# Trunk step in emulated fp32: norms in pairs of PSUM tiles, both statistics first, two output products in one step, a later mean

## The chip, the cores and the metric

The kernel runs on one core of one Trainium2 chip. The metric is device microseconds of one execution. Two other times occur: the *span* is the stretch of the profiled execution that the trace covers, and the time of that same execution is a little longer than its span. Engines are called by short names: PE (TensorE), DVE (VectorE), ACT (ScalarE), POOL (GpSimd), SP (SyncE, which issues the DMAs). L126 is line 126 of the kernel before.

## The reference

One layer of a decoder trunk on 1072 tokens (16 meta tokens, 1024 of a prompt, 8 x 4 new ones), 1024 channels wide, and then a last RMSNorm:

```python
def hybrid_layer(x, conv_prev, pool_prev, pos0, ...):
    x = x + 0.5 * swiglu(rmsnorm(x, g1), w1g, w1u, w1d)
    h = rmsnorm(x, gm)
    z = h @ w_in + b_in
    u = z[..., :C_CONV] * jax.nn.sigmoid(z[..., C_CONV:2 * C_CONV])
    p_in = z[..., 2 * C_CONV:]
    ...
    c = depthwise_causal_conv(u_ext, w_dw, b_dw)
    c = jax.nn.silu(layernorm(c, ln_g, ln_b))
    ...
    q = multiscale_pool(p_ext, pos0, w_pool, pool_scale)
    x = x + jnp.concatenate([c, q], axis=-1) @ w_out + b_out
    x = x + 0.5 * swiglu(rmsnorm(x, g2), w2g, w2u, w2d)
```

The hidden width of the SwiGLUs is 2816, the convolution is 31 wide and causal, the pools are trailing means over 2, 4, 8 and 16 positions, each with a 128 x 128 map. All is float32.

## The kernel before

**Layout.** Channels lie on the 128 partitions, tokens along the free dimension, so every product has weights as the stationary side and tokens as the moving side. The tokens are cut into three pieces of 358 columns, X1, X2 and X3 (tiles x_61, x_62 and x_4993 in the program's order; shorter where the padding of two columns, or the 16 meta tokens, are left away: 356 and 340). A number is held as a high and a low part, and each product is three matmuls (`mul`, L126): weight high by data high, weight high by data low, weight low by data high. `split` makes the two parts: ACT casts to the high part (L143), DVE subtracts it to get the low part (L144; POOL does this for weights, `wl`).

**PSUM.** One pool has eight banks, each an `acc` tile of 128 x 512. Matmul groups take them, and so do the norms, whose scaled tile lies in a bank between L265 and L144. A tile can be taken when the last instruction that reads its bank's earlier holder has run.

**Order.** PE's instructions run in the order in which the program writes them. The program is a plan of steps (one or a few products each, with weights fetched ahead through queues of raw and split tiles). Norms, mixings and operand sums are generators in the background: after each step of the plan `run_background` advances them by 1.8 of their `yield`s for each estimated microsecond of PE work; a `yield LAG` stops the front one until that much estimated PE time has gone by. A step that needs a generator's result runs it to its end at once (`got`, `finish`). Within DVE, ACT and POOL a scheduler sets the order from this program.

**The stages, and the generators that run beside them.** (1) first FFN of X1 and X2 together (a fast form with seven products in place of eight); (2) first FFN of X3, plain: beside it the norm `h1b` ahead of it, the norm `hma` of X1 and X2 for the first mixing, that mixing's input products (`proj_in`), its convolution, LayerNorm and pools (`mixer`), its output products (`proj_out`), and the norm `h2a`; (3) second FFN of X1 (340 columns), plain: beside it the norm `hmb` of X3 and the second mixing on X3, then `s2`, the operands of (4), the fast second FFN of X2 and X3, with seven operand pairs (b11, b21, t2, t3, t1, t4, b22) made by `fast_operands`; (5) the last norm.

**A norm** (`normed`) of a piece: squares on ACT, their adds on DVE (`square_sum`, L237), on PE a sum over partitions, an inverse root by small operations on DVE (`rsqrt`, L199 to L205), three diagonal tiles (L208, `diag`) which PE spreads over the partitions, a copy of that (`nr`, L217), and then for each of 8 channel tiles a scaled tile in PSUM (L265) and its split (L143, L144). Other names: `smt`, `mixl`, `mixh` and `mixlt` are the split results of norms and mixings, `hid0` to `hid2` hidden tiles of the FFNs, L489 the add of a down product to x, L515 a gate times its up product, L859 the LayerNorm's scaling and L843 its sum over channel tiles.

In the second mixing `conv_group` sums the convolution's channels, runs the pools, waits for LAG4 and then issues the mean's matmul (`mean_of`).

Of the kernel before, what the change touches and what calls it, by code (L numbers as in the profile page):

```python
# [2 lines left out]

# [9 lines left out]
ALU = mybir.AluOpType  # L13
# [40 lines left out]
LAG3 = 6.0  # L54
LAG4 = 7.0
LAG5 = 20.0
LAG6 = 4.0
POOL = {'b1': (1, 3), 't4': (0, 1, 2, 3), 't3': (0, 1, 2, 3), 't2': (1, 3), 'sq': ()}
W_BUFS = 6
T_BUFS = 6  # L60
# [24 lines left out]
def trunk(ctx: ExitStack, tc: tile.TileContext, xt, wf1, win, wout, wf2, wpool, vec, eye, sconv, spool,  # L85
# [34 lines left out]
    def accum():  # L120
        return pp.tile([P, 512], F32, name="acc", tag="acc")
# [19 lines left out]

    def split(hi, lo, src, engine=None):
        nc.scalar.copy(hi, src)  # L143
        (engine or nc.vector).tensor_tensor(lo, src, hi, ALU.subtract)  # L144


    raw_list = []
# [28 lines left out]
    def both_parts(w, k):  # L176

        wh, wl = w[k // KH]
        return wh[:, k % KH], wl[:, k % KH]
# [61 lines left out]
    def rms(piece, out):  # L241
        s = yield from square_sum([X(k, piece) for k in range(KD)])
        yield LAG
        out[piece] = yield from rsqrt(s, 1.0 / D, EPS)
# [19 lines left out]
    def scaled(t, piece, k, gain, r):  # L264
        nc.vector.scalar_tensor_tensor(t, X(k, piece), col(gain, k), r, ALU.mult, ALU.mult)  # L265

    def normed(pieces, gain, tiles, out, stats=None):

        st = {} if stats is None else stats
        h, lo = tiles()  # L270
        at = 0
        for piece in pieces:
            n = piece[1] - piece[0]
            if piece not in st:
                yield from rms(piece, st)
            for k in range(KD):
                t = accum()[:, :n]
                scaled(t, piece, k, gain, st[piece])
                yield
                split(h[:, k, at : at + n], lo[:, k, at : at + n], t)  # L280
                yield
            at += n
        out["h"] = (h, lo)
# [536 lines left out]
    def conv_group(piece, a0, cb, ch, cl, between, after):  # L820


        n = piece[1] - piece[0]
        npr = min(piece[1], END_PROMPT) - piece[0]
        if npr < n:
            us = mix["us"]
            taps = vecs[:, COL["w_dw"] : COL["w_dw"] + C_TILES * TAPS].rearrange("p (m k) -> p m k", m=C_TILES)
            cs = cb[:, :, npr:n].rearrange("p m (b t) -> p m b t", b=DEC_B)
            for t in range(DEC_T):
                for m in range(C_TILES):  # L830
                    pr = const.tile([P, DEC_B, TAPS], F32, name="pr", tag="tmp", bufs=T_BUFS)
                    nc.vector.tensor_tensor(pr, us[:, m, :, t : t + TAPS],  # L832
                                            taps[:, m : m + 1, :].broadcast_to([P, DEC_B, TAPS]), ALU.mult)
                    nc.vector.tensor_reduce(cs[:, m, :, t], pr, mybir.AxisListType.X, ALU.add)
                    yield
            for m in range(C_TILES):
                nc.vector.tensor_scalar(cb[:, m, npr:n], cb[:, m, npr:n], col("b_dw", m), None, ALU.add)
            yield
        s = const.tile([P, N], F32, name="ns", tag="ns")[:, :n]
        part = accum()[:, :n]  # L840
        nc.scalar.copy(part, cb[:, 0, :n])
        for m in (1, 2, 3):
            nc.vector.tensor_tensor(s if m == 3 else part, part, cb[:, m, :n], ALU.add)  # L843
            yield
        yield from between()
        yield LAG4
        mu = mean_of(s, 1.0 / (C_TILES * P), 0.0)
        yield
        for m in range(C_TILES):
            nc.vector.tensor_tensor(cb[:, m, :n], cb[:, m, :n], mu, ALU.subtract)  # L850
            yield
        s = yield from square_sum([cb[:, m, :n] for m in range(C_TILES)])
        yield LAG3
        yield from after()
        st = {}
        yield from rsqrt(s, 1.0 / (C_TILES * P), EPS, st, False)
        for m in range(C_TILES):
            t = accum()[:, :n]
            nc.vector.tensor_tensor(t, cb[:, m, :n], st["psum"], ALU.mult)  # L859
            nc.scalar.activation(t, t, AF.Silu, bias=col("ln_b", m), scale=col("ln_g", m))  # L860
            yield
            split(ch[:, m], cl[:, m], t)
            yield
# [67 lines left out]

    def proj_out(pieces, key):

        out = []
        for m in range(KD):
            def use(w, m=m):
                accs = [accum()[:, : b - a] for a, b in pieces]
                for what, ks in (("pool", range(C_TILES, KD)), ("h", range(C_TILES))):
                    h, lo = got(key, what)()
                    mul(accs, [(*both_parts(w, k), h[:, k], lo[:, k]) for k in ks], what == "pool", what == "h")  # L940
                for acc, piece in zip(accs, pieces):
                    nc.vector.scalar_tensor_tensor(X(m, piece), acc, col("b_out", m), X(m, piece), ALU.add, ALU.add)
            out.append(plain(wout[m], use))
        return out

    def store(piece, k, t):
# [446 lines left out]
```

## Time and profile before

| what | value |
|---|---|
| time, median of 3 runs | 1804.93 us (1803.71 to 1805.00) |
| time of the profiled execution | 1803.07 us |
| its span | 1801.3 us |
| granted TensorE clock, mean | 0.986 |
| PE busy | 1729.7 us (96%) |
| DVE busy | 1378.4 us (77%) |
| POOL busy | 1146.0 us (64%) |
| ACT busy | 760.3 us (42%) |

A busy time is the time in which the engine has an instruction in execution; its share is of the span. In a timeline, the first number is the start in microseconds from the span's start, the second how long the instruction (or a run of like ones, "x7") took, and brackets at the end hold the idle time of the engine ahead of it and the instruction that ended it. PEclk in a window is the granted clock as a share of full speed.

### The profile page before, as it was taken

Reading aid. Unit: us, or ns where it says so; the run is one execution under the profiler, and the core shown is the slowest. Engines: PE = TensorE matmul, PEld = TensorE weight load, DVE = VectorE, ACT = ScalarE, POOL = GpSimd, SP = SyncE. Lnnn points to the kernel's source line nnn. Section 1 sums busy time; section 2 is a strip of 40 time slices with the busy share of each in tenths; the row PEclk is TensorE's granted clock in tenths of the full one; section 3 lists DMA queues with packets and bytes.
Section 4 is the critical chain, followed back from the end, with each engine's and each line's share of the span. In section 5 each row is a group of like instructions: output and inputs, shape, how many; then the busy total and the mean of one; then the engine's idle time right before and its main releaser. Section 6 shows DMA issues by size and latency. Waiting matters only on the chain.

```text
span 1801.3 us, 29876 instructions
## 1 busy us (share of the span) xinstructions
PE 1729.7 (96%) x10486; PEld 1712.5 (95%) x10486; DVE 1378.4 (77%) x2621; ACT 760.3 (42%) x1482; POOL 1146.0 (64%) x894
## 2 busy tenths in 40 slices
PE   6799999999999999999999998999999999999997
PEld 6799999999999999999999998999999999999997
DVE  8869898989747795897235888538587989898965
ACT  6444444443435224434234433545353434444444
POOL 5576766667745337667346657666577676767683
PEclk9899999999999999999999999999999999999998
DMA  6122232223353223443234494444332222222232
GB/s 209 35 83 71 71 103 82 72 77 98 103 118 119 65 67 115 124 135 111 66 106 129 126 135 133 126 134 123 111 105 91 71 83 71 82 71 72 70 100 83
DMA packets 115893, 177.70 MB, mean 99 GB/s; under 512 B 28320, under 2 KB 35744, under 8 KB 115744
## 3 DMA queue, kind: packets, MB, share of 16 engines
q1 hardware_dynamic: 115744, 175.80, 33.4%
q8 instruction: 83, 1.36, 0.3%
q14 instruction: 66, 0.54, 0.1%
HBM read 170.60 MB, written 5.15 MB: 98 GB/s over the span
## 4 chain that ended last, share of the span: by engine, by line
PE 75%; DVE 17%; issue 4%; DMA 2%; POOL 1%; ACT 1%; SPq 0%; DVEq 0%; POOLq 0%; ACTq 0%
PE acc L126 75%; DMA wraw<-in_wf 2%; DVE acc L265 2%; POOL wl L144 1%; DVE acc L814 1%; DVE wraw L542 1%; DVE acc L570 1%; DVE wraw L541 1%; DVE tmp L570 1%; DVE tmp L692 1%; DVE x L489 1%; DVE tmp L265 1%; DVE pr L832 1%; DVE wraw L543 0%; DVE xb L144 0%
## 5 line engine op out<-in xcount | busy, mean ns | idle before, releaser
L144 POOL TENSOR_TENSOR wl<-wraw,wh 128x512 fp32r<-128x512 f32 x740 | 991.3, 1350 | 588.9 <-ACT wh L143 541.7
L143 ACT CAST wh<-wraw 128x512 fp32r<-128x512 f32 x740 | 453.6, 621 | 685.6 <-PE acc L126 455.5
L126 PE MATMUL acc<-smt,wh 128*128 128x358 f32 x1024 | 253.1, 328 | 5.0 <-DVE mixl L144 4.0
L126 PEld LDWEIGHTS acc<-smt,wh 128*128 128x128 f32 x1024 | 181.7, 190 | 6.3 <-DVE mixl L144 4.6
L814 DVE SCALAR_TENSOR_TENSOR acc<-ub,vecs,acc 128x340 f32<-128x340 f32 (+2 forms) x348 | 183.5, 571 | 2.6
L126 PE MATMUL acc<-mixlt,wh 128*128 128x340 f32 x704 | 165.6, 319 | 2.6 <-DVE smt L144 2.4
L126 PE MATMUL acc<-smt,wl 128*128 128x358 f32 x512 | 167.8, 328 | 0.0
L489 DVE SCALAR_TENSOR_TENSOR x<-acc,x 128x358 f32<-128x358 f32 (+1 forms) x240 | 119.4, 517 | 35.0 <-PE acc L126 34.2
L618 DVE SCALAR_TENSOR_TENSOR x<-acc,x 128x358 f32<-128x358 f32 x320 | 145.0, 516 | 0.5 <-PE acc L126 0.4
L570 DVE TENSOR_TENSOR acc<-tmp,acc 128x358 f32<-128x358 f32 x168 | 85.7, 527 | 51.5 <-PE acc L126 48.2
L126 PEld LDWEIGHTS acc<-mixlt,wh 128*128 128x128 f32 x704 | 120.9, 188 | 3.4 <-DVE smt L144 2.7
L126 PE MATMUL acc<-mixlt,wl 128*128 128x340 f32 x352 | 112.1, 319 | 0.8 <-POOL wl L144 0.8
L144 POOL TENSOR_TENSOR wl<-sx,wh 128x512 fp32r<-128x512 f32 x58 | 85.5, 1475 | 30.5 <-ACT wh L143 28.7
L126 PEld LDWEIGHTS acc<-smt,wl 128*128 128x128 f32 x512 | 96.9, 189 | 0.0
L542 DVE TENSOR_TENSOR wraw<-sx,wraw 128x512 f32<-128x512 f32 x58 | 78.1, 1347 | 11.8 <-POOL wl L144 11.6
L126 PE MATMUL acc<-mixh,wh 128*128 128x356 f32 (+1 forms) x320 | 79.3, 328 | 4.7 <-DVE mixl L144 2.7
L126 PE MATMUL acc<-mixl,wh 128*128 128x356 f32 (+1 forms) x320 | 78.6, 327 | 0.0
L126 PE MATMUL acc<-mixh,wl 128*128 128x356 f32 (+1 forms) x320 | 78.5, 327 | 0.0
L541 DVE TENSOR_TENSOR wraw<-wraw 128x512 f32<-128x512 f32 x58 | 77.0, 1327 | 0.4
L570 DVE TENSOR_TENSOR tmp<-tmp,acc 128x358 f32<-128x358 f32 x126 | 65.4, 519 | 14.3 <-PE acc L126 13.1
L126 PE MATMUL acc<-b11h,wh 128*128 128x358 f32 x184 | 61.7, 335 | 10.8 <-ACT wh L143 10.8
L543 DVE TENSOR_TENSOR wraw<-wraw 128x512 f32<-128x512 f32 x58 | 70.4, 1214 | 2.0 <-POOL wl L144 1.5
(286 smaller groups left out, 4762.1 us busy)
## 6 DMA issues: line engine op xcount, KB each, us to landing
wraw<-in_wf SPq DMA_DIRECT2D x544, 256.0 KB, 2.9
wraw<-in_win SPq DMA_DIRECT2D x48, 256.0 KB, 2.7
wraw<-in_wout SPq DMA_DIRECT2D x32, 256.0 KB, 2.9
x<-in_xt SPq DMA_DIRECT2D x8, 179.0 KB, 4.3
tmp<-in_xt SPq DMA_DIRECT2D x8, 179.0 KB, 2.8
x<-in_xt SPq DMA_DIRECT2D x1, 1432.0 KB, 7.0
x<-in_xt SPq DMA_DIRECT2D x8, 178.0 KB, 5.0
out_yt<-tmp SPq DMA_DIRECT2D x8, 170.0 KB, 3.3
```

Of the source, the lines that this page charges most:

```text
L126: tc.keep_in_program_order(nc.tensor.matmul(acc, lhs, rhs, start=start, stop=stop))
L143: nc.scalar.copy(hi, src)
L144: (engine or nc.vector).tensor_tensor(lo, src, hi, ALU.subtract)
L265: nc.vector.scalar_tensor_tensor(t, X(k, piece), col(gain, k), r, ALU.mult, ALU.mult)
L489: nc.vector.scalar_tensor_tensor(X(m, piece), acc, 0.5, X(m, piece), ALU.mult, ALU.add)
L541: nc.vector.tensor_tensor(a21, a11, a21, ALU.subtract)
L542: nc.vector.tensor_tensor(a11, s1, a11, ALU.subtract)
L543: nc.vector.tensor_tensor(a12, a12, a11, ALU.subtract)
L570: nc.vector.tensor_tensor(t, s, acc, ALU.add)
L618: nc.vector.scalar_tensor_tensor(to, acc, 0.5 * sign, to, ALU.mult, ALU.add)
L692: sub(t, t, ops[name][1][i], ALU.subtract)
L814: nc.vector.scalar_tensor_tensor(to, src, w, part, ALU.mult, ALU.add)
```

## The change

Four edits, none of which changes what is computed or how many instructions there are. (1) `normed` calls a new `rms_all`, which makes the statistics of all its pieces ahead of any scaled tile, and issues the first piece's `diag` matmul right after the second piece's squares; each scaled tile is queued on DVE behind the low part of two tiles before (`issue_after` sets an order within an engine and waits for nothing itself). (2) `proj_out` takes the first two output products in one step: pool parts of both, then the parts of the convolution group (`h`) of both. (3) In the second mixing the wait ahead of the mean's matmul is 14 and not 7 of estimated PE time. (4) The wait between two blocks of `fast_operands` is 9 and not 4. The new lines move later ones by 1, 2, 16 or more: L144 becomes L145, L208 becomes L209, L237 becomes L238, L265 becomes L266, L489 becomes L505 and L515 becomes L531.

```diff
-LAG6 = 4.0
+LAG6 = 9.0
+LAG7 = 14.0
...
     def split(hi, lo, src, engine=None):
         nc.scalar.copy(hi, src)
-        (engine or nc.vector).tensor_tensor(lo, src, hi, ALU.subtract)
+        return (engine or nc.vector).tensor_tensor(lo, src, hi, ALU.subtract)
...
+    def rms_all(pieces, out):
+
+        steps, last = None, None
+        for piece in pieces:
+            s = yield from square_sum([X(k, piece) for k in range(KD)])
+            if steps is not None:
+                out[last] = whole(steps)
+            yield LAG
+            steps, last = rsqrt(s, 1.0 / D, EPS), piece
+            next(steps)
+        if steps is not None:
+            yield LAG2
+            out[last] = whole(steps)
+
     def normed(pieces, gain, tiles, out, stats=None):
+
 
         st = {} if stats is None else stats
         h, lo = tiles()
-        at = 0
+        yield from rms_all([piece for piece in pieces if piece not in st], st)
+        at, lows = 0, []
         for piece in pieces:
             n = piece[1] - piece[0]
-            if piece not in st:
-                yield from rms(piece, st)
             for k in range(KD):
                 t = accum()[:, :n]
-                scaled(t, piece, k, gain, st[piece])
+                with tc.issue_after(lows[-2].ins) if len(lows) > 1 else nullcontext():
+                    scaled(t, piece, k, gain, st[piece])
                 yield
-                split(h[:, k, at : at + n], lo[:, k, at : at + n], t)
+                lows.append(split(h[:, k, at : at + n], lo[:, k, at : at + n], t))
                 yield
...
         yield from between()
-        yield LAG4
+        yield LAG4 if npr == n else LAG7
         mu = mean_of(s, 1.0 / (C_TILES * P), 0.0)
...
     def proj_out(pieces, key):
 
-        out = []
-        for m in range(KD):
-            def use(w, m=m):
-                accs = [accum()[:, : b - a] for a, b in pieces]
-                for what, ks in (("pool", range(C_TILES, KD)), ("h", range(C_TILES))):
-                    h, lo = got(key, what)()
-                    mul(accs, [(*both_parts(w, k), h[:, k], lo[:, k]) for k in ks], what == "pool", what == "h")
+
+        def products(w, m, accs, what, ks):
+            h, lo = got(key, what)()
+            mul(accs, [(*both_parts(w, k), h[:, k], lo[:, k]) for k in ks], what == "pool", what == "h")
+
+        def use(ws, ms):
+            banks = [[accum()[:, : b - a] for a, b in pieces] for _ in ms]
+            for what, ks in (("pool", range(C_TILES, KD)), ("h", range(C_TILES))):
+                for w, m, accs in zip(ws, ms, banks):
+                    products(w, m, accs, what, ks)
+            for m, accs in zip(ms, banks):
                 for acc, piece in zip(accs, pieces):
                     nc.vector.scalar_tensor_tensor(X(m, piece), acc, col("b_out", m), X(m, piece), ALU.add, ALU.add)
-            out.append(plain(wout[m], use))
+
+        out = []
+        for ms in ((0, 1), *((m,) for m in range(2, KD))):
+            out.append(("step", [[(0, wout[m])] for m in ms], lambda ms=ms: [unit() for _ in ms],
+                        lambda ws, ms=ms: use(ws, ms), False))
         return out
```

The rows of order that follow are the program's, without time; `x3` is a run of three like instructions.

DVE, norm `hmb` of X3 in the second mixing, from its diagonal tiles on, before:

```order
L208 TENSOR_SCALAR diag<-ident,few 128x128 x3
L489 SCALAR_TENSOR_TENSOR x_61<-acc,x_61 128x340 x3
L265 SCALAR_TENSOR_TENSOR acc<-x_4993,vecs,nr 128x358 x7
L144 TENSOR_TENSOR smt<-acc,smt 128x358 x7
L265 SCALAR_TENSOR_TENSOR acc<-x_4993,vecs,nr 128x358
L144 TENSOR_TENSOR smt<-acc,smt 128x358
L515 TENSOR_TENSOR acc<-acc,tmp 128x340
```

and of the change, the same place (the alternation goes on in this way to the eighth tile):

```order
L209 TENSOR_SCALAR diag<-ident,few 128x128 x3
L505 SCALAR_TENSOR_TENSOR x_61<-acc,x_61 128x340 x3
L266 SCALAR_TENSOR_TENSOR acc<-x_4993,vecs,nr 128x358 x2
L145 TENSOR_TENSOR smt<-acc,smt 128x358
L266 SCALAR_TENSOR_TENSOR acc<-x_4993,vecs,nr 128x358
L145 TENSOR_TENSOR smt<-acc,smt 128x358
L266 SCALAR_TENSOR_TENSOR acc<-x_4993,vecs,nr 128x358
L145 TENSOR_TENSOR smt<-acc,smt 128x358
```

Seven scaled tiles stood in a row before the first low part; now two do. The norms `hma` and `h2a` are changed in the same way.

DVE, norm `hma`, the first piece's root, while down products of X3 (`hid`) run on PE; before:

```order
L489 SCALAR_TENSOR_TENSOR x_4993<-acc,x_4993 128x358
L204 TENSOR_TENSOR acc<-acc,few 128x3
L205 SCALAR_TENSOR_TENSOR few<-acc,few 128x3
L489 SCALAR_TENSOR_TENSOR x_4993<-acc,x_4993 128x358
L208 TENSOR_SCALAR diag<-ident,few 128x128 x3
L489 SCALAR_TENSOR_TENSOR x_4993<-acc,x_4993 128x358 x3
L265 SCALAR_TENSOR_TENSOR acc<-x_61,vecs,nr 128x356 x7
L144 TENSOR_TENSOR mixl<-acc,mixh 128x356 x7
```

and of the change:

```order
L238 TENSOR_TENSOR acc<-acc,tmp 128x358
L205 TENSOR_TENSOR acc<-acc,few 128x3
L505 SCALAR_TENSOR_TENSOR x_4993<-acc,x_4993 128x358
L238 TENSOR_TENSOR ns<-acc,tmp 128x358
L206 SCALAR_TENSOR_TENSOR few<-acc,few 128x3
L204 SCALAR_TENSOR_TENSOR acc<-acc,few 128x3
L205 TENSOR_TENSOR acc<-acc,few 128x3
L206 SCALAR_TENSOR_TENSOR few<-acc,few 128x3
L204 SCALAR_TENSOR_TENSOR acc<-acc,few 128x3
L205 TENSOR_TENSOR acc<-acc,few 128x3
L206 SCALAR_TENSOR_TENSOR few<-acc,few 128x3
L209 TENSOR_SCALAR diag<-ident,few 128x128 x3
```

The square-adds of the second piece (L238) now stand ahead of the root's last operations and of its diagonal tiles, and the next x adds behind them.

PE at the same root, before:

```order
L126 MATMUL acc<-hid1h,wh 128x358
L126 MATMUL acc<-hid1l,wh 128x358
L126 MATMUL acc<-hid1h,wl 128x358
L126 MATMUL acc<-diag,ones 128x128 x3
L126 MATMUL acc<-smt,wh 128x358 x2
L126 MATMUL acc<-smt,wl 128x358
L126 MATMUL acc<-smt,wh 128x358 x2
```

and of the change:

```order
L127 MATMUL acc<-hid1h,wh 128x358
L127 MATMUL acc<-hid1l,wh 128x358
L127 MATMUL acc<-hid1h,wl 128x358
L127 MATMUL acc<-diag,ones 128x128 x3
L127 MATMUL acc<-hid0h,wh 128x358
L127 MATMUL acc<-hid0l,wh 128x358
```

The `diag` matmul stood at the end of the second half of the down products and stands now between the two halves: 24 matmuls earlier. The second piece's `diag` matmul stood 130 rows behind the first's, and stands 74 rows behind it.

DVE, operands of the second fast FFN, second block, up to the first x add of a down product; before:

```order
L144 TENSOR_TENSOR t2l<-acc,t2h 128x358
L329 TENSOR_TENSOR acc<-tmp,acc 128x358
L318 TENSOR_TENSOR tmp<-tmp,acc 128x358
L319 TENSOR_TENSOR acc<-acc,tmp 128x358
L265 SCALAR_TENSOR_TENSOR tmp<-x_62,vecs,nr 128x358
L144 TENSOR_TENSOR b11l<-tmp,b11h 128x358
L144 TENSOR_TENSOR b22l<-tmp,b22h 128x358
L265 SCALAR_TENSOR_TENSOR tmp<-x_62,vecs,nr 128x358
L515 TENSOR_TENSOR acc<-acc,tmp 128x340
L489 SCALAR_TENSOR_TENSOR x_61<-acc,x_61 128x340
```

and of the change:

```order
L145 TENSOR_TENSOR t2l<-acc,t2h 128x358
L345 TENSOR_TENSOR acc<-tmp,acc 128x358
L145 TENSOR_TENSOR b11l<-tmp,b11h 128x358
L145 TENSOR_TENSOR b22l<-tmp,b22h 128x358
L266 SCALAR_TENSOR_TENSOR acc<-x_4993,vecs,nr 128x358
L531 TENSOR_TENSOR acc<-acc,tmp 128x340
L145 TENSOR_TENSOR t4l<-acc,t4h 128x358
L505 SCALAR_TENSOR_TENSOR x_61<-acc,x_61 128x340
```

From the `hid1l` ahead of this stretch to that x add 22 instructions stood between; now 19 do.

## Rows read from the trace of the kernel before

**Rows 1.** The page: busy time by engine; costliest groups (busy us, mean ns).

```profile
PE 1729.7 (96%) x10486; PEld 1712.5 (95%) x10486; DVE 1378.4 (77%) x2621; ACT 760.3 (42%) x1482; POOL 1146.0 (64%) x894
...
L143 ACT CAST wh<-wraw 128x512 fp32r<-128x512 f32 x740 | 453.6, 621 | 685.6 <-PE acc L126 455.5
```

**Rows 2.** Timeline of PE: start, busy us, instruction, [idle before, releaser].

```profile
555.80 0.60 PE L126 MATMUL acc<-smt,wh 128*128 128x358 f32 x2 [2.20 <-DVE mixl L144]
...
587.59 0.86 PE L126 MATMUL acc<-mixh,wh 128*128 128x356 f32 x2 [2.66 <-DVE mixl L144]
...
947.31 0.60 PE L126 MATMUL acc<-smt,wh 128*128 128x358 f32 x2 [1.06 <-DVE mixlt L144]
...
996.78 0.58 PE L126 MATMUL acc<-mixlt,wh 128*128 128x340 f32 x2 [2.40 <-DVE smt L144]
```

**Rows 3.** Timeline of DVE, norm of the second mixing's tiles.

```profile
991.16 5.13 DVE L265 SCALAR_TENSOR_TENSOR acc<-x,vecs,nr 128x358 f32<-128x358 f32 x7 [0.65 <-ACT nr L217]
...
996.20 3.14 DVE L144 TENSOR_TENSOR smt<-acc,smt 128x358 fp32r<-128x358 f32 x7
```

**Rows 4.** Windows: length, busy PE, PEld, DVE, ACT, POOL; PEclk, DMA, GB/s.

```profile
588.00:592.00 4.00, 3.99 (x17) 3.97 (x17) 3.54 (x8) 0.90 (x2) 1.05 (x1) 0.65 0.25 81
...
997.00:1001.00 4.00, 4.00 (x27) 4.00 (x27) 3.47 (x9) 2.02 (x5) 2.74 (x2) 1.00 0.42 126
...
1244.00:1248.00 4.00, 3.33 (x12) 3.33 (x13) 4.00 (x10) 1.66 (x4) 2.27 (x2) 0.57 0.31 82
```

**Rows 5.** Timeline of PE, where the first mixing's root is due.

```profile
544.90 0.32 PE L126 MATMUL acc<-hid0h,wh 128*128 128x358 f32 x1
...
548.85 0.83 PE L126 MATMUL acc<-diag,ones 128*128 128x128 f32 x6
```

**Rows 6.** Timeline of DVE around that root, and square-adds behind it.

```profile
541.05 0.17 DVE L199 TENSOR_SCALAR acc<-acc 128x3 f32<-128x3 f32 x1
541.26 0.17 DVE L200 TENSOR_SCALAR acc<-acc 128x3 int32<-128x3 int32 x1
...
545.10 0.53 DVE L489 SCALAR_TENSOR_TENSOR x<-acc,x 128x358 f32<-128x358 f32 x1 [0.19 <-PE acc L126]
...
546.53 0.92 DVE L208 TENSOR_SCALAR diag<-ident,few 128x128 f32<-128x128 f32 x3
...
558.78 1.10 DVE L237 TENSOR_TENSOR acc<-acc,tmp 128x358 f32<-128x358 f32 x2
```

**Rows 7.** Timeline of PE, operands of the second fast FFN.

```profile
1244.67 0.65 PE L126 MATMUL acc<-hid0h,wh 128*128 128x340 f32 x1 [2.67 <-DVE x L489]
...
1266.13 0.42 PE L126 MATMUL acc<-hid0l,wh 128*128 128x340 f32 x1 [1.31 <-DVE hid0l L144]
```

**Rows 8.** Timeline of DVE, operands of the second fast FFN.

```profile
1230.69 0.80 DVE L265 SCALAR_TENSOR_TENSOR tmp<-x,vecs,nr 128x358 f32<-128x358 f32 x1
...
1232.41 0.52 DVE L318 TENSOR_TENSOR tmp<-tmp,acc 128x358 f32<-128x358 f32 x1
1232.85 1.44 DVE L144 TENSOR_TENSOR b22l<-tmp,b22h 128x358 fp32r<-128x358 f32 x1
...
1244.12 0.50 DVE L489 SCALAR_TENSOR_TENSOR x<-acc,x 128x340 f32<-128x340 f32 x1
```

**Rows 9.** Timeline of PE, first output product of the first mixing.

```profile
859.28 0.43 PE L126 MATMUL acc<-mixh,wh 128*128 128x358 f32 x1 [2.06 <-ACT mixh L143]
```

**Rows 10.** Timelines of PE and DVE, end of the second mixing.

```profile
1161.07 0.83 PE L126 MATMUL acc<-diag,ones 128*128 128x128 f32 x6
...
1167.56 0.52 DVE L144 TENSOR_TENSOR smt<-acc,smt 128x358 fp32r<-128x358 f32 x1
...
1172.97 0.48 PE L126 MATMUL acc<-smt,wh 128*128 128x358 f32 x2
```

**Rows 11.** Timeline of DVE, one tile of the second FFN's norm.

```profile
949.70 0.56 DVE L265 SCALAR_TENSOR_TENSOR acc<-x,vecs,nr 128x340 f32<-128x340 f32 x1
...
950.77 0.51 DVE L144 TENSOR_TENSOR mixlt<-acc,mixlt 128x340 fp32r<-128x340 f32 x1 [0.51 <-ACT mixlt L143]
```

More of the change, by code (lines that the diff above doesn't have):

```diff
@@ L1 @@
 from collections import deque
-from contextlib import ExitStack
+from contextlib import ExitStack, nullcontext
 import concourse.bass as bass
```

## The prediction

> **What bounds the kernel now.** The page comes first: PE is busy 96% of the span [rows 1], so the change, which leaves every matmul in place, can only return idle time of PE or add some. I next took the list of PE's waits, then its timeline at each wait to see which instruction of another engine came last, then that engine's timeline to see why, and last the windows behind each wait, for the granted clock.
>
> In the norms PE waits four times for a low part, 2.20, 2.66, 1.06 and 2.40 us [rows 2]. The matmul that waits is no user of that low part: it is the first of a product that needs a PSUM bank. The reason stands on DVE: seven scaled tiles run in a row for 5.13 us, then seven low parts for 3.14 us [rows 3]. A bank is free again only when its low part has run, so seven of eight banks are held for 5 us while PE's products ask for new ones. The clock is the second price: in the 4 us behind the wait of 2.66 it is granted at 0.65, with 17 matmuls in place of about 24 (24 matmuls of 358 columns take 548.85 − 544.90 = 3.95 us, 0.164 each [rows 5]); behind the 2.40 it stays at 1.00 [rows 4]. A dip costs 7 x 0.164 = 1.2 us.
>
> In the operands of the second fast FFN PE waits 2.67 us for an x add and 1.31 for a low part of a hidden tile [rows 7]: there DVE is simply behind. The add comes at 1244.12, after 13.4 us of operand work without a pause [rows 8]. The window behind it has a clock of 0.57 [rows 4].
>
> **The change part by part.**
>
> *Pairs of PSUM tiles.* No instruction is added. DVE now does scaled and low in turn, 0.73 + 0.45 = 1.18 us for a tile [rows 3]. Does a low part have to wait for its cast? Alone, a low part starts 0.51 us after its scaled tile ends [rows 11]; in the new order another low part and another scaled tile, 1.18 us, lie between, so 0.67 us is to spare, and a 0.62 us weight cast of ACT in between [rows 1] just fits. Two to three banks are held in place of seven. I take all four waits away: 2.20 + 2.66 + 1.06 + 2.40 = 8.3 us, and the one dip 1.2: **−9.5**. Bounds: 0 if something holds the banks anyway, −9.5 if all goes.
>
> *Both statistics first.* Here lies the cost. In the first mixing's norm the first piece's diagonal matmul moves from the end of a half of down products to its beginning, 24 matmuls earlier: before, PE came to it at 548.85 and its diagonals had begun at 546.53 [rows 5, 6], so it never waited. Now PE is there at 544.90. What has to be over by then on DVE? The order puts four x adds, with a square-add behind each, ahead of the root's last seven small operations. The fourth x add stands behind the product that ends the half, so it starts no earlier than 545.10 [rows 6]. From there: 0.5 for the add, 0.5 for the square-add (1.10 for two [rows 6]), seven small operations at a pitch of 0.21 (541.05 to 541.26 [rows 6]), 1.5, one diagonal 0.31 (0.92 for three): 547.9 with nothing late, a wait of 3.0. But each x (0.5), square-add (0.5) and the small operation between them (0.2) make 1.2 us, against six matmuls of PE, 0.98: over four of them DVE falls back by about 1 us. So I take **+4.0**, bounds 2.9 and 4.7 (the later with more backlog). Work that covers it: none, the matmul stands in PE's queue, with the other half of the down products behind it. Behind waits of 2.66 and 2.67 the clock dipped, behind 2.40 not [rows 2, 4, 7]; I add a dip, **+1.2**, bounds 0 and 1.7. The second piece's root has 74 rows of PE work between, over 12 us, for some 13 small operations: no wait. The norms of one piece have no second statistic to move.
>
> *First two output products together.* In the first mixing PE waits 2.06 us for the cast `mixh` ahead of the h part of the first product [rows 9]. Its chain starts at a diagonal matmul that stands directly ahead of the h parts, now as before, so the pool parts of the second product come before the diagonal, not between it and the wait. The wait only moves: 0. Bounds ±2: it may vanish, or double if banks for four accumulators come late.
>
> *Later mean, second mixing.* The mean's matmul moves back by 48 matmuls; there was no wait before it. What shrinks is the cover at the end: from the diagonal to the first h product lay 72 matmuls of hidden and `mixlt` products (1161.07 to 1172.97, 11.9 us [rows 10]) and 12 of the pool part (0.164 each, 2.0), 13.9 us; now it is 24 (a third of the 11.9, 4.0) and 24 of pool parts (both products', since they are paired, 3.9), 7.9 us. The last low part started 6.5 us after the diagonal [rows 10], and took 0.5. It fits by 0.9 only, so I take **+0.5**, bounds 0 and 1.5: what would be late is the last two h products, and nothing but PE waits for them.
>
> *Longer wait between operand blocks.* Of 22 DVE instructions between `hid1l` and the late x add, 19 remain, about 0.6 each (13.4 us for 22 [rows 8]): the add comes 1.8 us sooner, of the 2.67 that PE waited. The hidden tile's low part now follows its gate product by 4 rows, not 12, so its 1.31 goes. A shorter wait should lose the dip. 1.8 + 1.3 + 1.2: **−4.3**, bounds 0 and −5.2 (all of it). Operand blocks that come later press on the start of the fast pass; the last block had its slack there, as PE shows no wait at it.
>
> **Sum.** −9.5 + 5.2 + 0.5 − 4.3 = −8.1 against the profiled execution, 1803.07, gives 1795.0; the median of the runs lies 1.86 above that, 1804.93 − 8.1 = **1796.8**.
>
> **The rivals.**
>
> *DVE stays late in the operands.* Operations of DVE with both inputs in SBUF can be held up: `b22l` took 1.44 us where an operation of the same size with one input in PSUM took 0.52 just before [rows 8], while POOL works 64% of the time [rows 1]. With two such hold-ups in another place, 1.8 us, the three instructions saved are eaten, and all of the 5.2 stays: −9.5 + 5.2 + 0.5 = −3.8, **1801.1**; with one more hold-up each in the root's chain, where x adds and square-adds are of mixed kinds, 1802. For it: the row. Against it: most of the 22 took 0.52. The Trainium skill, "SBUF — State Buffer", section "🔬 SBUF: two separate sides", states that VectorE and GpSimd share a pair of ports as a lock, held for a whole instruction, when a VectorE operation has two SBUF inputs and GpSimd reads SBUF, and that the loser waits in full; the long row agrees (a POOL weight subtraction began at about the same time), and by that rule the place of a hold-up follows the new order and can't be read from before.
>
> *The new root wait is short.* If the scheduler's order leaves DVE ahead, or the matmul finds work enough before it: −9.5 − 4.3 + 0.5 = −13.3, **1791.6**. Against it: the fourth x add's 545.10 is bound to PE's own product, and the chain behind it is serial.
>
> *The pace of two tiles becomes the bound: slower.* With seven tiles ahead a late cast cost nothing; with two it stops DVE, and PE needs the last tiles of each norm. If a tile takes t in place of 1.18 us, the 16, 8 and 8 tiles of three norms come 32 (t − 1.18) later, of which some 10 us is slack before their products. To end 0.2% above the time before, 8.1 + 3.6 = 11.7 us must come of it: t = 1.18 + 21.7/32 = 1.86. The chain alone, without overlap, takes 1.58 (949.70 to 950.77 and 0.51 [rows 11]), so every tile would need a wait behind a weight cast. At t = 1.86 the time is **1808.5**.
>
> **How the numbers follow.** Forecast 0.65; operands stay late 0.17; short root wait 0.11; slower pace 0.07. A difference of 0.2%, 3.6 us, is about what a measurement of this kernel can tell from no change: faster means under 1801.3, slower over 1808.5. The forecast's own bounds reach from 1793 to 1801; it holds nearly all its chance under 1801.3. The operands' case lies about that bound, 0.07 of it under. So faster 0.80 (0.62 + 0.07 + 0.11), same 0.13, slower 0.07. The range for 8 in 10 runs from 1791.0, which takes in the short root wait, to 1802.0, which takes in the late operands.
>
> **What would show it.** The four waits for `mixl`, `mixlt` and `smt` are gone from PE's list, and DVE's rows read two scaled tiles, then low and scaled in turn at about 1.2 us. At about 545 PE waits 3 to 5 us for `diag`, with a clock near 0.6 behind it. The wait for `mixh` is still about 2 us. The wait for the x add falls under 1 us or so. The new wait ahead of the second mixing's h products is under 1.5. The prediction is wrong if `diag` doesn't wait, if PE waits in its place for a low part at the input products (`mixl` too late, not banks too few), or if the x add is as late as now.

## The result

The change is faster: median 1793.93 us (1793.74 to 1794.99, 4 runs) against 1804.32 (1803.42 to 1805.00, 4 runs), a ratio of 0.9942 with a 95% interval of 0.9928 to 0.9957. That is 10.4 us, where 8.1 were forecast. Run again on another chip, beside other kernels, it had 0.9956 (0.9943 to 0.9969), which is nearer to the forecast. The profiled execution has a span of 1792.2 us, 9.1 under that of before. Busy times hardly moved, as they should where no instruction is added; on the page of the change:

```profile
PE 1726.9 (96%) x10486; PEld 1710.3 (95%) x10486; DVE 1384.0 (77%) x2621; ACT 759.7 (42%) x1482; POOL 1146.5 (64%) x894
```

PE's waits tell what moved. Of the list of PE's waits after (engine and line waited for: us in total, times, longest):

```profile
PE acc L127 <- DVE diag L209: 14.0, 4, 7.5
...
PE acc L127 <- DVE x L505: 5.0, 4, 2.7
...
PE acc L127 <- DVE mixl L145: 1.8, 1, 1.8
```

The waits for low parts of [rows 2] are gone; the 1.8 us left for `mixl` stand at the convolution (before: 1.76 at 823.90), which the change didn't touch. `diag` has a fourth wait. x adds hold PE up four times, 5.0 us in all. Where these are, on PE's timeline of the change:

```profile
547.09 0.91 PE L127 MATMUL acc<-diag,ones 128*128 128x128 f32 x6 [2.92 <-DVE diag L209]
...
574.36 0.43 PE L127 MATMUL acc<-hid2h,wh 128*128 128x358 f32 x1 [1.40 <-DVE x L505]
...
859.85 0.43 PE L127 MATMUL acc<-mixh,wh 128*128 128x358 f32 x1 [2.06 <-ACT mixh L144]
...
1239.02 0.42 PE L127 MATMUL acc<-hid0h,wh 128*128 128x340 f32 x1 [0.62 <-DVE x L505]
...
1263.63 0.42 PE L127 MATMUL acc<-hid2h,wh 128*128 128x340 f32 x1 [2.71 <-DVE x L505]
```

The wait of 2.92 answers to [rows 5]: a wait where there was none. The 1.40 stands in place of the two `mixl` waits of the first mixing. The 2.06 for `mixh` is the one of [rows 9], moved behind 24 more matmuls. The last two answer to [rows 7]: 0.62 in place of 2.67, but a new 2.71.

On DVE, the norm `hmb` after, to be held against [rows 3]:

```profile
986.62 1.61 DVE L266 SCALAR_TENSOR_TENSOR acc<-x,vecs,nr 128x358 f32<-128x358 f32 x2 [0.65 <-ACT nr L218]
988.25 0.53 DVE L145 TENSOR_TENSOR smt<-acc,smt 128x358 fp32r<-128x358 f32 x1
988.70 0.59 DVE L266 SCALAR_TENSOR_TENSOR acc<-x,vecs,nr 128x358 f32<-128x358 f32 x1
989.20 0.52 DVE L145 TENSOR_TENSOR smt<-acc,smt 128x358 fp32r<-128x358 f32 x1
...
991.52 1.49 DVE L266 SCALAR_TENSOR_TENSOR acc<-x,vecs,nr 128x358 f32<-128x358 f32 x1
...
994.80 1.14 DVE L145 TENSOR_TENSOR smt<-acc,smt 128x358 fp32r<-128x358 f32 x2
```

Scaled and low alternate as the order said. The eight tiles take 9.3 us (986.62 to 995.94), 1.17 each, close to the 1.18 that was forecast; before, the eight took 9.8 (991.16 to 1000.91). Where nothing is held up a tile takes 0.95 (988.25 to 989.20), as the next start follows 0.45 or 0.50 after a start although 0.53 or 0.59 is listed; but one of the scaled tiles took 1.49.

To see where time was won and lost, the same matmul is read in both traces. Of before:

```profile
823.90 0.59 PE L126 MATMUL acc<-smt,wh 128*128 128x358 f32 x2 [1.76 <-DVE mixl L144]
...
1073.96 0.43 PE L126 MATMUL acc<-mixlt,wl 128*128 128x340 f32 x1 [0.77 <-POOL wl L144]
...
1308.54 0.43 PE L126 MATMUL acc<-t2h,wl 128*128 128x358 f32 x1 [1.01 <-POOL wl L144]
...
1687.85 0.43 PE L126 MATMUL acc<-hid0h,wh 128*128 128x358 f32 x1 [1.22 <-ACT cc L668]
...
1788.41 0.83 PE L126 MATMUL acc<-ones,q1h 128*128 128x1 f32 x6 [1.72 <-DVE q1h L1245]
```

and of the change:

```profile
820.64 0.59 PE L127 MATMUL acc<-smt,wh 128*128 128x358 f32 x2 [1.77 <-DVE mixl L145]
...
1067.36 0.52 PE L127 MATMUL acc<-mixlt,wl 128*128 128x340 f32 x1 [0.78 <-POOL wl L145]
...
1300.81 0.43 PE L127 MATMUL acc<-t2h,wl 128*128 128x358 f32 x1 [0.77 <-POOL wl L145]
...
1679.99 0.43 PE L127 MATMUL acc<-hid0h,wh 128*128 128x358 f32 x1 [1.23 <-ACT cc L684]
...
1779.35 0.83 PE L127 MATMUL acc<-ones,q1h 128*128 128x1 f32 x6 [1.72 <-DVE q1h L1269]
```

The lead (how much earlier the change has the same matmul) is 3.3 us behind the first mixing's norm, 6.6 behind the two norms that follow, 7.7 behind the operands, and it holds to 1688 (7.9). The rest, to 9.1, comes between 1688 and 1788, where the change did nothing: there the trace of before has a window at a clock of 0.57 and that of the change, at the same work, one at 1.00.

```profile
1688.00:1692.00 4.00, 4.00 (x16) 4.00 (x17) 3.79 (x10) 2.27 (x5) 2.69 (x3) 0.57 0.10 30
```

```profile
1680.00:1684.00 4.00, 4.00 (x24) 4.00 (x25) 3.80 (x9) 2.42 (x5) 2.54 (x3) 1.00 0.09 19
```

So of the 9.1 us between the two profiled executions 1.2 come from a place that the change doesn't touch. The clock also goes against the change: behind its wait at 1067.36 it has a window at 0.63, with 19 matmuls, where the execution of before stayed at 1.00 behind 1073.96.

```profile
1068.00:1072.00 4.00, 4.00 (x19) 4.00 (x19) 3.62 (x8) 3.20 (x7) 4.00 (x4) 0.63 0.90 313
```

A microsecond or two between two executions can be the clock alone; the medians below are the firmer measure.

### The profile page after: what moved, and what is told of

The parts are those of the page before. It is cut to its first block, busy times and chain, and to the rows that moved or that the text cites. A ratio compares the mean times of both kernels' runs of the same rounds, so it can differ in the third digit from the quotient of the medians.

```text
span 1792.2 us, 29876 instructions
## 1 busy us (share of the span) xinstructions
PE 1726.9 (96%) x10486; PEld 1710.3 (95%) x10486; DVE 1384.0 (77%) x2621; ACT 759.7 (42%) x1482; POOL 1146.5 (64%) x894
## 4 chain that ended last, share of the span: by engine, by line
PE 73%; DVE 19%; issue 3%; DMA 2%; ACT 1%; POOL 1%; SPq 0%; DVEq 0%; POOLq 0%; ACTq 0%
PE acc L127 73%; DMA wraw<-in_wf 2%; DVE wraw L558 1%; DVE acc L586 1%; DVE tmp L586 1%; DVE acc L830 1%; DVE wraw L557 1%; DVE tmp L708 1%; DVE acc L266 1%; DVE tmp L266 1%; DVE x L505 1%; POOL wl L145 1%; DVE pr L848 1%; DMA x<-in_xt 0%; DVE cc L716 0%
## 5 line engine op out<-in xcount | busy, mean ns | idle before, releaser
L145 POOL TENSOR_TENSOR wl<-wraw,wh 128x512 fp32r<-128x512 f32 x740 | 992.5, 1353 | 581.1 <-ACT wh L144 539.3
L144 ACT CAST wh<-wraw 128x512 fp32r<-128x512 f32 x740 | 452.9, 621 | 662.7 <-PE acc L127 438.8
L505 DVE SCALAR_TENSOR_TENSOR x<-acc,x 128x358 f32<-128x358 f32 (+1 forms) x240 | 119.3, 516 | 35.6 <-PE acc L127 34.9
L145 POOL TENSOR_TENSOR wl<-sx,wh 128x512 fp32r<-128x512 f32 x58 | 85.0, 1465 | 29.8 <-ACT wh L144 28.0
```

The lines of the kernel that those rows point to most:

```text
L145: return (engine or nc.vector).tensor_tensor(lo, src, hi, ALU.subtract)
L505: nc.vector.scalar_tensor_tensor(X(m, piece), acc, 0.5, X(m, piece), ALU.mult, ALU.add)
```

## The experiments

Each kernel was timed beside the kernel before on its chip; the ratio to that, with its interval, is what can be compared between groups of runs. The first four ran together, the next four, and the last four.

| run | median us | ratio to before, 95% interval |
|---|---|---|
| the change | 1793.93 | 0.9942 (0.9928 to 0.9957) |
| stats_in_turn | 1790.37 | 0.9921 (0.9907 to 0.9934) |
| no_pairs | 1799.53 | 0.9970 (0.9959 to 0.9982) |
| root_later | 1793.55 | 0.9942 (0.9929 to 0.9954) |
| lag6_undone | 1796.24 | 0.9956 (0.9943 to 0.9968) |
| mean_undone | 1795.98 | 0.9961 (0.9949 to 0.9973) |
| single_products | 1798.98 | 0.9975 (0.9966 to 0.9985) |
| turn_t3_psum | 1790.53 | 0.9929 (0.9915 to 0.9943) |
| turn_lag6_mid | 1792.18 | 0.9935 (0.9920 to 0.9950) |
| change_again | 1794.34 | 0.9956 (0.9943 to 0.9969) |
| mean_products_undone | 1795.09 | 0.9962 (0.9949 to 0.9975) |
| pairs_lag6 | 1789.17 | 0.9926 (0.9913 to 0.9939) |
| pairs_only | 1789.67 | 0.9929 (0.9916 to 0.9942) |

**stats_in_turn.** In `normed` of the change:

```diff
-        yield from rms_all([piece for piece in pieces if piece not in st], st)
...
             n = piece[1] - piece[0]
+            if piece not in st:
+                yield from rms(piece, st)
```

> The change with one part undone: each piece's statistics stand again ahead of its own tiles, the pairs of PSUM tiles stay. Theory (the pairs give the whole gain in the norms, the statistics together cost a wait): the wait for diag at about 547 (2.92 us) and the wait for an x add at 574 (1.40) go and nothing comes in their place, so about 4.3 us less than the change, near 1789.6. Rival (the statistics together are needed, since with pairs the second piece's tiles would come too late behind its own root): PE waits for mixl at the first input product, 2.5 us or more, and the time is 1793 or above.

The theory held: 1790.37, against 1789.6 expected, with no wait for `diag` near 547 and none for an x add near 574. Of its timeline of PE, all that waits in the first mixing's norm:

```profile
582.47 0.43 PE L127 MATMUL acc<-mixh,wh 128*128 128x358 f32 x1 [0.51 <-DVE mixl L145]
```

A half microsecond stands in place of 2.92 and 1.40 (and of 2.20 and 2.66 before). Pairs of tiles alone are enough there; the statistics together are a loss.

**no_pairs.** In `normed` of the change:

```diff
-                with tc.issue_after(lows[-2].ins) if len(lows) > 1 else nullcontext():
-                    scaled(t, piece, k, gain, st[piece])
+                scaled(t, piece, k, gain, st[piece])
```

> The change with one part undone: scaled tiles are no longer queued behind the low part of two tiles before, the statistics together stay. Theory (seven held banks made PE wait): seven scaled tiles stand in a row again and the waits for low parts of about 1 to 2.7 us are back in all three norms, 8 to 9 us with a dip of the clock, near 1803. Rival (the order of the statistics took the waits away, banks are not short): within 2 us of the change, 1792 to 1796.

1799.53: between the two. PE's timeline says why:

```profile
548.48 0.91 PE L127 MATMUL acc<-diag,ones 128*128 128x128 f32 x6 [2.92 <-DVE diag L209]
...
944.78 0.59 PE L127 MATMUL acc<-smt,wh 128*128 128x358 f32 x2 [1.06 <-DVE mixlt L145]
...
994.25 0.58 PE L127 MATMUL acc<-mixlt,wh 128*128 128x340 f32 x2 [2.40 <-DVE smt L145]
```

In the norms of one piece the waits of 1.06 and 2.40 are back to the hundredth, so there the pairs are the cause. That it is banks that the pairs set free is read from the traces, where the matmul that waits is no user of the low part; no run changed the number of banks. In the first mixing no `mixl` wait came back: with the statistics together DVE's order has at most four scaled tiles in a row there, without any pairing. So each of the two edits by itself takes away the first mixing's waits; together they do it once (the pairs leave 0.51 us, as stats_in_turn shows), and the statistics add their own cost.

**root_later.** In `rms_all` of the change:

```diff
             if steps is not None:
+                yield 3.0
                 out[last] = whole(steps)
```

> The change, with a wait of 3.0 of estimated PE time ahead of the first piece's diagonal matmul, so that it stands behind both halves of the down products as before. Theory (the new wait for diag is only a matter of its place): the 2.92 us go, the diag is ready when PE comes to it, and the norm's tiles have slack: near 1791.0. Rival (the whole norm moves back by the same time and its tiles are late): a wait for mixl or x at 574 to 590 takes its place, 1793 to 1796.

Neither as put: 1793.55, the rival's number, but the wait is again for `diag`:

```profile
551.68 1.54 PE L127 MATMUL acc<-diag,ones 128*128 128x128 f32 x6 [2.01 <-DVE diag L209]
```

The three diagonals behind that wait are on DVE:

```profile
550.34 1.68 DVE L209 TENSOR_SCALAR diag<-ident,few 128x128 f32<-128x128 f32 x3
```

The matmul came 24 matmuls later, 3.95 us. The diagonals began 3.7 us later than in the change (550.34 against 546.66), of which 1.5 is the lag of this whole execution by then (the low part `hid2l` at 542.67 against 541.13). The other 2.1 are new: on DVE the root's small operations now stand one or two behind each x add of the second half, and the last of them behind an x add at 549.70 that waited for PE. And the diagonals took 1.68 us where they took 0.68 in the change. So the wait shrank by 0.9 and not by 2.92: the root's end follows the down products' x adds wherever the matmul is put. The wait of 1.40 for an x add at 574 went, with 0.34 for `mixl` in its place; still the median is that of the change. In the profiled execution the clock took some of it back (0.59 in the 4 us from 552, 1.00 in the change behind its wait).

**lag6_undone.** `LAG6 = 9.0` in the change is `LAG6 = 4.0` again.

> The change with the wait between operand blocks at 4 again. Theory (the trace after: x-add waits of 0.62, 0.31 and 2.71 us in place of 2.67 and 1.31 with a dip, so the longer wait gives net 1.5 to 2 us): 1795.4 to 1796. Rival one (the forecast's 4.3 us, of which other places took some back): near 1798.2. Rival two (the longer wait only moves the lateness to a later block): same as the change within 0.7 us.

1796.24, 2.3 over the change's median, by ratio 0.0014 x 1804 = 2.5; the intervals overlap. That is a little above the theory's range. The two waits of [rows 7] are back:

```profile
1240.24 0.42 PE L127 MATMUL acc<-hid0h,wh 128*128 128x340 f32 x1 [2.66 <-DVE x L505]
...
1261.77 0.42 PE L127 MATMUL acc<-hid0l,wh 128*128 128x340 f32 x1 [1.31 <-DVE hid0l L145]
```

Together 3.97, against 0.31 + 0.62 + 2.71 = 3.64 us in the change. The sum of waits hardly differs: the longer wait moved them, as rival two has it. What it gave beyond that is the clock, 0.57 in the 4 us from 1240 here, with 14 matmuls, and 1.00 from 1236 to 1252 in the change.

**mean_undone** and **single_products**, each on the change:

```diff
-        yield LAG4 if npr == n else LAG7
+        yield LAG4
```

```diff
-        for ms in ((0, 1), *((m,) for m in range(2, KD))):
+        for ms in ((m,) for m in range(KD)):
```

> The change with the mean of the second mixing at its earlier place (the wait at 7 for both mixings). Theory (nothing waited for the mean before and nothing waits for the later scaling behind it in the trace after): same as the change, 1793.2 to 1794.7. Rival (the forecast's step: the last h products come late by 0.5 us or more because the cover shrank, so the earlier place is better): 1792 to 1793.3.

> The change with the first two output products as steps of their own again, in both mixings. Theory (the wait of 2.06 us for mixh only moves with the diagonal matmul, and the second mixing has no wait there): same as the change, 1793.2 to 1794.7, with mixh still at about 2.06 us. Rival (pairing hides part of the casts behind the pool parts of the second product): 1 to 2 us slower, near 1795.5.

The first came out at 1795.98, but the twelve runs spread from 1793.74 to 1802.18 and the kernel before from 1799.12 to 1808.36 on that chip: unclear by time; the profiled execution took 1793.74 us, that of the change 1794.0. The second took 1798.98, slower than either side expected: its interval lies above that of the change, and just touches that of change_again. In its trace the wait for `mixh` is 2.06 as before, so the first mixing is as forecast. A loss stands in the second, where no wait had been, at the h parts of the first product (a pair of `smt,wh` matmuls takes 0.49 when nothing is late):

```profile
1170.72 1.00 PE L127 MATMUL acc<-smt,wh 128*128 128x358 f32 x2
1171.72 0.87 PE L127 MATMUL acc<-smt,wh 128*128 128x358 f32 x2
1172.74 0.99 PE L127 MATMUL acc<-smt,wh 128*128 128x358 f32 x2
```

0.51 + 0.38 + 0.50 = 1.4 us lost in waits for h parts. With the mean later and the products single, only 24 `mixlt` matmuls and 12 of the pool part lie between the diagonal (1164.23) and the first h product, 6.5 us, and the last low part ends 9.5 us behind the diagonal (1173.69), not 7.0 as in [rows 10]: with the mean later, squares on ACT and square-adds on DVE (L238) of a norm run ahead of the low parts and between them. It is so in the change too:

```profile
1162.53 0.83 PE L127 MATMUL acc<-diag,ones 128*128 128x128 f32 x6
```

```profile
1171.01 0.97 DVE L145 TENSOR_TENSOR smt<-acc,smt 128x358 fp32r<-128x358 f32 x2 [0.18 <-ACT smt L144]
```

Its last low part also ends 9.5 us behind the diagonal (1171.98), and its first h product starts 8.3 behind it (1170.85), but the fourth low part is first read by the pair of matmuls at 1172.35, so nothing waits. The 1.4 us are not all that single_products lost; in its profiled execution the clock is 0.63 from 548 and 0.60 from 1268, where the change has 1.00, and whether that has to do with the edit isn't shown.

**mean_products_undone.** Both of these edits at once, on the change.

> The change with two parts undone together: output products one at a time, and the mean at its earlier place. Theory (the later mean takes away cover that the pairing of products gives back: alone, single products left gaps of PE of some 1.5 us at the second mixing's h products): without both, no such gaps and the same time as the change within 0.8 us on the same chip. Rival (pairing the products is worth something by itself): 1 us or more slower than the change.

1795.09 against 1794.34 for change_again on its chip, ranges overlapping: the theory held, and in the trace no h product is late. The pairing of products gives back the cover that the later mean takes; the two together are worth nothing that can be measured.

**turn_t3_psum**, on stats_in_turn:

```diff
-            t3 = temp()[:, :n]
+            t3 = accum()[:, :n]
             sub(t3, b22, t, ALU.subtract)
```

> Statistics in turn as in the run stats_in_turn, and in the operands of the second fast FFN the difference t3 lies in a PSUM bank and no longer in SBUF, so its low part has one PSUM input. Theory (what makes DVE late there is operations with two SBUF inputs that are held up while POOL works: t3l took 1.29 us on average where t1l with a PSUM input took 0.52): t3l falls to 0.52, four blocks win 0.8 us each, the wait for the x add of 2.72 us shrinks to under 1.5, and the time is 1 to 2.5 us under 1790.4. Rival one (the next operation with two SBUF inputs takes the hold-up over): another low part or scaled tile is long in its place and the time stays at 1790.4 within 0.7. Rival two (a bank more for each block is what PE lacks): new waits for low parts, 1791 or above.

The time is that of rival one, and the traces show its sign and also that of rival two. Groups of DVE between 1180 and 1300 of stats_in_turn (count | busy us, mean ns of one | idle before):

```profile
L145 DVE TENSOR_TENSOR t3l<-tmp,t3h 128x358 fp32r<-128x358 f32 x4 | 5.1, 1287 | 0.0
...
L145 DVE TENSOR_TENSOR b22l<-tmp,b22h 128x358 fp32r<-128x358 f32 x4 | 3.2, 795 | 0.0
L145 DVE TENSOR_TENSOR b11l<-tmp,b11h 128x358 fp32r<-128x358 f32 x4 | 2.5, 637 | 0.6 <-ACT b11h L144 0.6
L145 DVE TENSOR_TENSOR b21l<-tmp,b21h 128x358 fp32r<-128x358 f32 x4 | 2.3, 572 | 0.0
```

and with t3 in PSUM:

```profile
L145 DVE TENSOR_TENSOR b11l<-tmp,b11h 128x358 fp32r<-128x358 f32 x4 | 4.9, 1214 | 0.6 <-ACT b11h L144 0.6
L145 DVE TENSOR_TENSOR b22l<-tmp,b22h 128x358 fp32r<-128x358 f32 x4 | 4.2, 1061 | 0.0
L145 DVE TENSOR_TENSOR b21l<-tmp,b21h 128x358 fp32r<-128x358 f32 x4 | 3.2, 793 | 0.0
...
L145 DVE TENSOR_TENSOR t3l<-acc,t3h 128x358 fp32r<-128x358 f32 x4 | 2.1, 517 | 0.0
```

`t3l` fell from 1287 to 517 ns, as low as every other subtraction with a PSUM input, and the three low parts that still have two SBUF inputs became longer: b11l rose from 637 to 1214. The four together took 13.1 us before and 14.4 after; scaled tiles, whose inputs are both in SBUF too, fell from 15.1 to 12.9. Of the 3.1 us that t3l gave (4 x 0.77), 0.9 was left. The time stayed at 1790.53. The wait of 2.72 for the x add did go, as the theory has it, but others came, the first of them for a low part in PSUM, which had been 0.31:

```profile
1232.38 0.42 PE L127 MATMUL acc<-hid0h,wh 128*128 128x340 f32 x1 [2.32 <-DVE t4l L145]
```

With 0.24 and 1.05 for casts of hidden tiles behind it that makes 3.6 us, as much as before (0.31 + 0.62 + 2.72). Whether `t4l` is late for want of a bank or for the two long low parts ahead of it on DVE (1.51 and 1.59) isn't separated.

What the long operations have in common can be read from the trace of stats_in_turn. A long one, on DVE, and what ran beside it on POOL:

```profile
1246.73 1.62 DVE L145 TENSOR_TENSOR b22l<-tmp,b22h 128x358 fp32r<-128x358 f32 x1
```

```profile
1245.12 2.84 POOL L145 TENSOR_TENSOR wl<-wraw,wh 128x512 fp32r<-128x512 f32 x2 [2.01 <-ACT wh L144]
```

Of the 16 low parts with two SBUF inputs between 1180 and 1300, the 6 that began while POOL had an instruction running took 0.74 to 1.63 us, the other 10 took 0.51 to 0.52. The 33 additions and subtractions of this shape with a PSUM input that the timeline lists one by one took 0.51 to 0.54, though 18 of them began beside POOL. With t3 in PSUM 7 of 12 low parts with two SBUF inputs began beside POOL, and those took 0.91 to 1.62.

**turn_lag6_mid**, on stats_in_turn: `LAG6 = 6.5`.

> Statistics in turn as in the run stats_in_turn, and the wait between operand blocks at 6.5 in place of 9. Theory (the total of operand work is the same, a longer wait moves DVE's lateness from the second block to the fourth): waits of about 1.5 us at both places, within 0.7 us of 1790.4. Rival (in between, both blocks have slack): no wait over 1 us there and 1788 to 1789.

1792.18 (1788.84 to 1793.54), 0.9935: no faster, and neither as put. The waits were 2.66 at the second block and 1.32 for the hidden tile's low part, none at the fourth: as at 4, not in between.

**change_again, pairs_lag6, pairs_only.** The change itself; stats_in_turn with mean and products undone too; and that with LAG6 at 4.

> The change itself, for a comparison with the three kernels beside it on the same chip. Both theories: 0.994 of the time before, 1793 to 1795, with waits of 2.92 for diag, 1.40 and 2.71 for x adds.

> Only two parts of the change: pairs of PSUM tiles with each piece's statistics ahead of its own tiles, and the longer wait between operand blocks. Theory (the other parts cost or give nothing): the same as stats_in_turn, 3 to 4.5 us under the change on the same chip, near 1790. Rival (pairing and later mean are worth something): 1791.5 or above.

> Only one part of the change: pairs of PSUM tiles, each piece's statistics ahead of its own tiles. Theory (norm waits are 9.5 us and more with the one ahead of the second FFN's X3, the wait between operand blocks gives 2 to 2.7): 10 to 12 us under the time before, 1792 to 1794, with the x-add wait of 2.7 and the hidden tile's 1.3 back. Rival (the gain in the norms needs the statistics together): 1796 or above.

On one chip: 1794.34, 1789.17 and 1789.67, the last 2.3 us under what was expected; change_again has its waits of 2.92, 1.40 and 2.71 as expected. The pairs of PSUM tiles alone give more than the whole change. The longer wait between operand blocks adds 0.5 us to that, within the spread (1788.13 to 1790.77 and 1788.73 to 1790.70). pairs_only has the old waits at the operands, 1.31 for the hidden tile's low part at 1253.70 and this one:

```profile
1232.20 0.43 PE L127 MATMUL acc<-hid0h,wh 128*128 128x340 f32 x1 [2.68 <-DVE x L506]
```

## Why the prediction was right, and where it was off

The time lies in the range, and both large terms have the sign and the place that were forecast. Four kernels that were timed on one chip beside the kernel before take the change apart (the runs of each spread over 2 to 4 us, those of before over 7, so the small steps are not clear of noise):

| step, and the medians that it lies between | forecast us | measured us |
|---|---|---|
| pairs of tiles (before 1802.02, pairs_only 1789.67) | −9.5 | −12.4 |
| longer wait between blocks (to pairs_lag6, 1789.17) | −4.3 | −0.5 |
| both statistics first (to mean_products_undone, 1795.09) | +5.2 | +5.9 |
| later mean, and first two products together (to change_again, 1794.34) | +0.5 | −0.8 |
| sum | −8.1 | −7.7 |

That the sum came out so near is luck in part: the pairs gave 2.9 us more than forecast and the longer wait 3.8 less. Point by point:

*Pairs of tiles, −9.5.* Right in mechanism and too small: pairs_only is 12.4 us under before (0.9929, 10.5 to 15.1 by its interval), and in the norms of one piece no_pairs brought the very waits back. The forecast left out 0.48 us of `h1b`, which also went, and 0.51 that stayed; the other 3 us are not taken apart. In the profiled executions the clock has a share in them: before has windows at 0.59 from 824 and 0.57 from 1688, and pairs_only has 1.00 at the same work. What the forecast had not seen is that the statistics together would also have removed the first mixing's waits. The rival of a slower pace is refuted: 1.17 us for a tile, not 1.86.

*Both statistics first, +5.2.* Right in mechanism and in sum, wrong in its parts. The step that was mis-sized is the wait, "+4.0, bounds 2.9 and 4.7": it was 2.92, near the 3.0 "with nothing late". The lost microsecond of backlog was not there, because an x add, a square-add and the small operation behind them, put at 1.2 us, take 0.94 together (543.45 to 544.39), which fits into six matmuls of 0.98. In DVE's timeline of the change:

```profile
543.45 0.52 DVE L505 SCALAR_TENSOR_TENSOR x<-acc,x 128x358 f32<-128x358 f32 x1
...
544.39 0.52 DVE L505 SCALAR_TENSOR_TENSOR x<-acc,x 128x358 f32<-128x358 f32 x1
544.83 0.52 DVE L238 TENSOR_TENSOR ns<-acc,tmp 128x358 f32<-128x358 f32 x1
...
546.66 0.68 DVE L209 TENSOR_SCALAR diag<-ident,few 128x128 f32<-128x128 f32 x3
```

The next starts 0.44 after the last though each is listed with 0.52. The dip of the clock for which 1.2 was added did not follow in the profiled execution of the change, but it did in four of the seven executions with this wait. A cost that was not foreseen was there: 1.40 for an x add, which stands on DVE behind scaled tiles and low parts that run without a pause from 561 to 573. So the waits make 2.92 + 1.40 − 0.51 (the wait that stays without this part) = 3.8, and with a dip of 1.4 us 5.2. The medians give 5.9 (mean_products_undone minus pairs_lag6, which differ only in the statistics) and 3.6 (the change minus stats_in_turn, timed in different groups).

*First two products together, 0, and the later mean, +0.5.* The wait for `mixh` moved and stayed at 2.06, and nothing waits at the second mixing's h products. But the cover did not suffice in the way that was worked out: the last low part ended 9.5 us behind the diagonal, not 7.0, and came in time because it is read last of the four. Without the pairing 1.4 us of waits came.

*Longer wait between blocks, −4.3.* The term that was off. In the traces the lead is 5.9 us at the last long wait ahead of this stretch (3.84 us at 1111.26 before, 3.83 at 1105.36 after) and 7.7 at 1308.54, so 1.8 were won, and the medians give 0.5 to 2.5. What the term counted did happen: 0.31 and 0.62 in place of the 2.67, no wait in place of the 1.31, no dip. The failed step is "the last block had its slack there, as PE shows no wait at it": the blocks that came later put 2.71 us of wait for an x add at 1263.63. That DVE stays late there was the first rival; its mechanism, operations with two SBUF inputs, is at work (`t3l` 1287 ns against 517), and turn_t3_psum showed what makes it hard to cure, that other such operations became long instead.

## What to carry to other kernels

Count the buffers that a run of like instructions holds before its first consumer runs: seven scaled tiles in a row for eight banks stopped an engine that used none of them, and an order of two at a time cost nothing (9.3 us for eight tiles, 9.8 before). When several edits go in together, do each alone: here one part gave 12 us on its chip, and another gave 4 to 6 of them back. A later start for background work moved its lateness to a later consumer here, as its sum of work stayed the same.

## What the runs showed of the hardware

The clock behind a wait was not fixed by the wait. The same wait of 2.92 us for `diag` stands in seven of the profiled executions. In three of them (the change, change_again, mean_undone) the clock stayed at 1.00 behind it; in four (no_pairs, lag6_undone, single_products, mean_products_undone) it fell to 0.62 to 0.66 in the window from 548, a mean over 4 us of its two levels, 2.4 and 1.2 GHz. Of the change and of lag6_undone:

```profile
548.00:552.00 4.00, 4.00 (x26) 4.00 (x26) 1.60 (x4) 1.21 (x3) 1.29 (x1) 1.00 0.03 7
```

```profile
548.00:552.00 4.00, 3.97 (x18) 4.00 (x19) 0.80 (x3) 0.46 (x1) 0.00 (x0) 0.62 0.18 66
```

From the `diag` matmul to the next one that waits, near 575, it was 27.3 us with the full clock and 28.7 with the dip: 1.4 us that a forecast can only put as a chance.

A DVE operation with two SBUF inputs took 0.5 to 1.6 us for one and the same shape, where those with one PSUM input had means of 514 to 526 ns; when one of them was taken out of SBUF, others became long in its place. The Trainium skill, "SBUF — State Buffer", section "🔬 SBUF: two separate sides", states an exclusive lock between VectorE with two SBUF inputs and GpSimd; the runs agree with it in which operations are long (`t3l` 1287 ns from SBUF, 517 from PSUM) and in when (all 6 low parts that began while POOL worked, none of the 10 others). No run took POOL's subtractions away.
